# Mean over rows of 8192 on one core: a loop's 8 MB loads issued by GpSimd through the software queue

## The chip, the cores and the metric

The kernel runs on one core of a Trainium2 chip. A core has engines with instruction streams of their own: VectorE (DVE in the profile), ScalarE (ACT), GpSimd (POOL), SyncE (SP) and TensorE, which this kernel doesn't use. Sixteen DMA engines move data between the memory outside (HBM) and the core's on-chip memory (SBUF, 128 partitions). Engines issue DMAs; when one has landed, it raises a semaphore by 16, one for each DMA engine. The metric is the device time of one execution in microseconds (us), given as the median of several runs.

## What is computed

```python
def setup_inputs():
    return {"x": np.random.randn(64, 256, 8192).astype(np.float32)}

def reference(x):
    return np.mean(x, axis=2)
```

The input is 16,384 rows of 8192 floats, 536.9 MB; the output is one mean for each row, 64 KB. Each number is read once and added once.

## The kernel before

Rows are dealt to partitions so that a partition's rows lie one behind the other in memory: each partition owns 128 rows, 111 in a first zone and 17 in a second. A row is 32 KB, so one row for every partition is 4 MB. There are two landing buffers, `two` (two rows for each partition, 8 MB over all) and `four` (four rows, 16 MB).

The work goes through these buffers in turn. Ahead of the loop SyncE loads two single rows into `two` (three DMAs, lines 110 to 112) and four rows into `four` (line 113). Then come 17 rounds (`ROUNDS`) of six rows: two into `two` (line 117), four into `four` (line 119). Behind the loop stand five more loads of the same two sizes (`REST`, lines 122 to 128), two more 8 MB loads, and the last two rows in six pieces that get smaller and smaller.

All loads are issued by SyncE, in the order in which they are wanted, into one hardware queue. Ahead of each load SyncE waits until its buffer is free: for `two` until `two_free` is at least 1, which it then lowers by 1 (line 116); for `four` until `four_free` is at least 2, which it lowers by 2 (line 118).

VectorE sums the rows. `pair` (lines 169 and 170) sums both rows of `two` in one instruction and raises `two_free`. `quad` (lines 172 to 176) sums three rows of `four`, each by a `halves` (line 152) that adds the halves of a row and accumulates the result. ScalarE sums the fourth row of `four` at the same time (line 220, called in line 228). Both raise `four_free`.

VectorE's order is fixed by its program: in every round it waits for `two_sem` (line 184), does `pair`, waits for `go_sem`, which ScalarE raises when `four` has landed (lines 187 and 226), does `quad`, and copies three sums from a small tile to their place (line 190). So it takes `two` and `four` strictly in turn, whichever has landed.

GpSimd has little to do: at its start it raises `turn_sem`, and near the end it scales the first zone's 111 sums by 1/8192 (line 92, once `four_free` has reached 4), and later 16 of the second zone's (line 98).

Of the kernel before, what the change touches and what calls it, by code (L numbers as in the profile page):

```python
# [6 lines left out]
ADD = mybir.AluOpType.add  # L7
X = mybir.AxisListType.X
# [3 lines left out]
def bass_global_avg_pool_1d_kernel(  # L12
# [6 lines left out]
    B, C, L = x.shape  # L19
# [7 lines left out]
    ZONE = [111, 17]  # L27
    FROM = [0, ZONE[0]]
    EARLY, LATE = ZONE
    ROUNDS = (ZONE[0] - 9) // 6  # L30
# [16 lines left out]
    zone = [  # L47
        flat[P * f : P * (f + n), :].rearrange("(p r) l -> p (r l)", p=P)
        for f, n in zip(FROM, ZONE)
    ]  # L50
# [5 lines left out]
    with ExitStack() as ctx:  # L56
        sb = lambda n, s: ctx.enter_context(nc.sbuf_tensor(n, s, F32))
        sem = lambda n: ctx.enter_context(nc.semaphore(n))
# [8 lines left out]
        two = sb("two", [P, 2 * L])  # L67
# [3 lines left out]
        two_sem = sem("two_sem")  # L71
        turn_sem = sem("turn_sem")
        four_free = sem("four_free")
        two_free = sem("two_free")
# [4 lines left out]
        last_sem = sem("last_sem")  # L79
        pool_sem = sem("pool_sem")  # L80
        late_sem = sem("late_sem")
        out_sem = sem("out_sem")

        tail = four[:, 2 * L : 4 * L]
# [1 line left out]

        eng = nc.gpsimd
        eng.sem_inc(turn_sem, 2)  # L90
        eng.wait_ge(four_free, 4)
        eng.tensor_scalar(  # L92
            scaled[:], res[:, 0:EARLY], inv, None, op0=mybir.AluOpType.mult
# [8 lines left out]


        eng = nc.sync
        def rows_of(n, k):
            z = 1 if n >= FROM[1] else 0
            return zone[z][:, (n - FROM[z]) * L : (n - FROM[z] + k) * L]

        a, z = rows_of(ZONE[0] - 1, 1), rows_of(ZONE[0], 1)
        eng.dma_start(two[:, L : L + FIRST], z[:, 0:FIRST]).then_inc(first_sem, 16)  # L110
        eng.dma_start(two[:, L + FIRST : 2 * L], z[:, FIRST:L]).then_inc(first_sem, 16)
        eng.dma_start(two[:, 0:L], a).then_inc(first_sem, 16)
        eng.dma_start(four[:], rows_of(0, 4)).then_inc(second_sem, 16)
        src = rows_of(4, 6 * ROUNDS).rearrange("p (i w) -> p i w", i=ROUNDS)
        with eng.Fori(0, ROUNDS) as i:
            eng.wait_ge(two_free, 1).then_inc(two_free, -1)
            eng.dma_start(two[:], src[:, bass.ds(i, 1), 0 : 2 * L]).then_inc(two_sem, 16)
            eng.wait_ge(four_free, 2).then_inc(four_free, -2)
            eng.dma_start(four[:], src[:, bass.ds(i, 1), 2 * L : 6 * L]).then_inc(
                four_sem, 16  # L120
            )
# [12 lines left out]
        for c in range(6):  # L134
            a, z = cuts[c], cuts[c + 1]
# [12 lines left out]
        eng = nc.vector  # L148
# [16 lines left out]
        rows_in = lambda ap: ap.rearrange("p (j l) -> p j l", l=L)  # L165
        at = lambda n, k: res[:, n : n + k]
        sums = res[:, 4 : 4 + 6 * ROUNDS].rearrange("p (i w) -> p i w", i=ROUNDS)

        def pair(to, ap=two[:]):
            eng.tensor_reduce(to, rows_in(ap), X, ADD).then_inc(two_free, 1)  # L170

        def quad(to, done=four_free):
            for j, ap in enumerate(to):
                halves(
                    four[:, j * L : (j + 1) * L], ap, done if j == len(to) - 1 else None
                )

        eng.wait_ge(first_sem, 48)
        pair(at(ZONE[0] - 1, 2))
        eng.wait_ge(second_sem, 16)  # L180
        quad([at(j, 1) for j in range(3)])
        with eng.Fori(0, ROUNDS) as i:
            now = sums[:, bass.ds(i, 1), :]
            eng.wait_ge(two_sem, 16).then_inc(two_sem, -16)  # L184
            pair(now[:, :, 0:2])
            eng.wait_ge(go_sem, 1).then_inc(go_sem, -1)
            eng.wait_ge(turn_sem, 2).then_inc(turn_sem, -2)  # L187
            quad([turn[:, j : j + 1] for j in range(3)], turn_sem)
            eng.wait_ge(turn_sem, 1).then_inc(four_free, 1)
            eng.tensor_copy(  # L190
                now[:, :, 2:5], turn[:].rearrange("p (i w) -> p i w", i=1)
            ).then_inc(turn_sem, 1)
        for k, (n, size) in enumerate(REST):
            eng.wait_ge(two_sem if size == 2 else four_sem, 16 * (k // 2 + 1))
            if size == 4:
                quad([at(n, 1), at(n + 1, 1)])
            elif k < len(REST) - 1:
                pair(at(n, 2))
            else:
                pair(at(n, 1), two[:, 0:L])  # L200
# [16 lines left out]
        eng = nc.scalar  # L217
# [20 lines left out]
        for c in range(4):  # L238
            eng.wait_ge(chunk_sems[c], 16)
            a = cuts[c] if c else L  # L240
            ap = tail[:, a : a + mine[c]]
# [29 lines left out]
```

## Time and profile before

| what | value |
|---|---|
| time, median of 3 runs | 1243.4 us (1242.87 to 1243.65) |
| time of the profiled execution | 1242.81 us |
| its span in the profile | 1241.5 us |
| VectorE busy | 643.0 us |
| ScalarE busy | 176.6 us |
| GpSimd busy | 0.9 us |
| data moved | 536.94 MB, mean 433 GB/s |

The span runs from the first to the last recorded work; the device time has some 1.3 us more around it. In the profile's rows L152 is line 152 of the kernel; "SPq" is the instruction stream of SyncE, where DMA issues and waits stand. Of a DMA issue the profile gives the line, the buffer it writes and reads (`two<-in_x_dram`), how many there were, and the median time from issue to landing. A group's row gives what it wrote and read, the number of instructions, the busy time, the mean of one, and the idle time ahead of them with what ended it.

### The profile page before, as it was taken

The page shows a single profiled execution, that of the slowest core. Times are in us where ns is not written, and L with a number is a line of the kernel's source. Part 1 is how long each engine was busy: PE and PEld are TensorE (multiplying, and loading weights), DVE is VectorE, ACT ScalarE, POOL GpSimd, SP SyncE. Part 2 cuts the span into 40 slices and gives each one's busy share as a digit, 9 for nine tenths or more (in the row PEclk, how much of TensorE's full clock was granted, in tenths as well). Part 3 has the DMA queues.
Part 4 walks back from the last instruction along what each step waited for, and adds up shares of the span by engine and source line. Part 5 has one row for each costly group of instructions (what it writes and reads, how often), then busy time and mean ns, then how long its engine had stood idle before and what let it go on. Part 6 is the DMA issues. An engine that isn't in the chain of part 4 may idle for free. (4 is left out here: it accounts for less than half of the span.)

```text
span 1241.5 us, 715 instructions
## 1 busy us (share of the span) xinstructions
DVE 643.0 (52%) x168; ACT 176.6 (14%) x57; POOL 0.9 (0%) x6
## 2 busy tenths in 40 slices
DVE  2373836454544637383736454554638383725257
ACT  0011020202020202012020202020202102040423
POOL 0000000000000000000000000000000000000000
DMA  9999999999999999999999999999999999999998
GB/s 405 439 439 439 439 429 416 439 439 439 439 439 422 422 439 439 439 439 439 416 429 439 439 439 439 439 410 435 439 439 439 439 439 408 437 439 439 439 439 374
DMA packets 10192, 536.94 MB, mean 433 GB/s; under 512 B 1104, under 2 KB 1488, under 8 KB 1616
## 3 DMA queue, kind: packets, MB, share of 16 engines
q1 hardware_dynamic: 10192, 536.94, 99.9%
HBM read 536.87 MB, written 0.07 MB: 433 GB/s over the span
## 5 line engine op out<-in xcount | busy, mean ns | idle before, releaser
L152 DVE CUSTOM_DVE_ANT_0 four<-four 128x4096 f32<-128x4096 f32 (+4 forms) x63 | 260.7, 4184 | 434.9 <-DVEq L187 366.9
L170 DVE TENSOR_REDUCE res<-two 128x16384 f32 (+2 forms) x21 | 353.1, 16814 | 145.1 <-DVEq L184 96.2
L220 ACT ACTIVATE four<-four 128x8192 f32<-128x8192 f32 x22 | 154.7, 7030 | 1017.8 <-ACTq L226 864.3
L202 DVE TENSOR_REDUCE res<-four 128x2 f32<-128x16384 f32 x1 | 17.2, 17219 | 10.7 <-DMA four<-in_x_dram 10.7
L220 ACT ACTIVATE two<-two 128x8192 f32<-128x8192 f32 x2 | 14.1, 7032 | 36.7 <-DMA two<-in_x_dram 36.7
L206 DVE TENSOR_REDUCE res<-two 128x1 f32<-128x8192 f32 x1 | 8.7, 8686 | 2.1 <-DMA two<-in_x_dram 2.1
L242 ACT ACTIVATE four<-four 128x1984 f32<-128x1984 f32 (+3 forms) x4 | 4.3, 1064 | 7.8 <-DMA four<-in_x_dram 7.8
L190 DVE COPY res<-turn 128x3 f32 x17 | 2.9, 169 | 4.2 <-DVE turn L152 4.2
L152 DVE DVE_READ_ACCUMULATOR2_ANT turn<- 128x1 f32 x51 | 4.2, 82 | 0.0
L220 ACT ACTIVATION_READ_ACCUMULATOR four<-four (+1 forms) x22 | 4.1, 187 | 0.0
L220 ACT ACT_TABLE_LOAD x1 | 1.3, 1283 | 0.7 <-PEq L256 0.7
L92 POOL TENSOR_SCALAR scaled<-res 128x111 f32<-128x111 f32 x1 | 0.5, 505 | 1118.0 <-ACT four L220 1118.0
L242 ACT ACTIVATION_READ_ACCUMULATOR four<-four 128x1 f32 x4 | 0.8, 188 | 0.0
L152 DVE DVE_READ_ACCUMULATOR2_ANT res<- 128x1 f32 x8 | 0.7, 83 | 0.0
L220 ACT ACTIVATION_READ_ACCUMULATOR two<-two 128x1 f32 x2 | 0.4, 188 | 0.0
L98 POOL TENSOR_SCALAR ends<-res 128x16 f32<-128x16 f32 x1 | 0.3, 255 | 117.8 <-DVE res L152 117.8
L152 DVE DVE_READ_ACCUMULATOR2_ANT fin<- 128x1 f32 x4 | 0.3, 83 | 0.0
L152 DVE CUSTOM_DVE_ANT_0 fin<-fin 128x100 f32<-128x100 f32 x1 | 0.3, 264 | 0.0
L256 POOL MEMSET const-bfloat16-1.0<- 128x1 bf16 x1 | 0.1, 103 | 0.0
L256 POOL MEMSET const-uint8-127<- 128x1 uint8 x1 | 0.1, 102 | 0.0
L256 POOL MEMSET const-float32-0.0<- 128x1 f32 x1 | 0.1, 99 | 0.2 <-issue 0.2
L256 POOL MEMSET const-float32-1.0<- 128x1 f32 x1 | 0.1, 99 | 0.0
(1 smaller groups left out, 0.1 us busy)
## 6 DMA issues: line engine op xcount, KB each, us to landing
four<-in_x_dram SPq DMA_DIRECT2D x1, 5088.0 KB, 41.6
two<-in_x_dram SPq DMA_DIRECT2D x1, 4096.0 KB, 20.7
two<-in_x_dram SPq DMA_DIRECT2D x1, 3072.0 KB, 11.5
four<-in_x_dram SPq DMA_DIRECT2D x1, 2048.0 KB, 45.9
two<-in_x_dram SPq DMA_DIRECT2D x1, 1024.0 KB, 4.7
four<-in_x_dram SPq DMA_DIRECT2D x1, 640.0 KB, 47.0
four<-in_x_dram SPq DMA_DIRECT2D x21, 44.1
two<-in_x_dram SPq DMA_DIRECT2D x21, 40.3
```

The source lines that it names most:

```text
L92: eng.tensor_scalar(scaled[:], res[:, 0:EARLY], inv, None, op0=mybir.AluOpType.mult).then_inc(pool_sem, 1)
L98: eng.tensor_scalar(ends[:, 0 : LATE - 1], res[:, EARLY : OWN - 1], inv, None, op0=mybir.AluOpType.mult,).then_inc(late_sem, 1)
L152: made = eng.tensor_tensor_reduce(ap[:, 0:n], ap[:, 0:n], ap[:, n : 2 * n], scale=scale, scalar=0.0, op0=ADD, op1=ADD, accum_out=to,)
L170: eng.tensor_reduce(to, rows_in(ap), X, ADD).then_inc(two_free, 1)
L190: eng.tensor_copy(now[:, :, 2:5], turn[:].rearrange("p (i w) -> p i w", i=1)).then_inc(turn_sem, 1)
L202: eng.tensor_reduce(at(HALF, 2), rows_in(four[:, 0 : 2 * L]), X, ADD).then_inc(owned_sem, 1)
L206: eng.tensor_reduce(at(LASTP, 1), two[:, 0:L], X, ADD).then_inc(owned_sem, 1)
L220: return eng.activation(ap, ap, COPY, accum_out=to)
L242: eng.activation(ap, ap, COPY, accum_out=part(c)).then_inc(last_sem, 1)
L256: nc = _bacc.Bacc("TRN2", target_bir_lowering=False, num_devices=1)
```

## The change

GpSimd gets a loop of 17 rounds that issues the 8 MB loads of the loop, with `single_packet=True`: the eight runs of 64 KB that a DMA engine moves for such a load are marked as one packet. A DMA that GpSimd issues goes through the software queue. SyncE's loop keeps the 16 MB loads. Two semaphores are new: `loop_free`, which `pair` raises in the loop (and ahead of it) instead of `two_free`, and `soft_sem`, which the GpSimd loads raise. VectorE waits for `soft_sem` to reach 16 times the round's number, counted from 1, and doesn't lower it. After its loop GpSimd waits for the last `loop_free` and raises `two_free` by 1, so that SyncE's first 8 MB load behind the loop can start. All loads outside the loop stay with SyncE. What is loaded, where to, and how it is summed is the same.

```diff
+        loop_free = sem("loop_free")
+        soft_sem = sem("soft_sem")
...
+        def rows_of(n, k):
+            z = 1 if n >= FROM[1] else 0
+            return zone[z][:, (n - FROM[z]) * L : (n - FROM[z] + k) * L]
+
+        src = rows_of(4, 6 * ROUNDS).rearrange("p (i w) -> p i w", i=ROUNDS)
+
         eng = nc.gpsimd
         eng.sem_inc(turn_sem, 2)
+        with eng.Fori(0, ROUNDS) as i:
+            eng.wait_ge(loop_free, 1).then_inc(loop_free, -1)
+            eng.dma_start(
+                two[:], src[:, bass.ds(i, 1), 0 : 2 * L], single_packet=True
+            ).then_inc(soft_sem, 16)
+        eng.wait_ge(loop_free, 1)
+        eng.sem_inc(two_free, 1)
         eng.wait_ge(four_free, 4)
...
-        src = rows_of(4, 6 * ROUNDS).rearrange("p (i w) -> p i w", i=ROUNDS)
-        with eng.Fori(0, ROUNDS) as i:
-            eng.wait_ge(two_free, 1).then_inc(two_free, -1)
-            eng.dma_start(two[:], src[:, bass.ds(i, 1), 0 : 2 * L]).then_inc(two_sem, 16)
+        with eng.Fori(0, ROUNDS) as i:
             eng.wait_ge(four_free, 2).then_inc(four_free, -2)
             eng.dma_start(four[:], src[:, bass.ds(i, 1), 2 * L : 6 * L]).then_inc(
                 four_sem, 16
             )
...
-        def pair(to, ap=two[:]):
-            eng.tensor_reduce(to, rows_in(ap), X, ADD).then_inc(two_free, 1)
+        def pair(to, ap=two[:], free=two_free):
+            eng.tensor_reduce(to, rows_in(ap), X, ADD).then_inc(free, 1)
...
-        pair(at(ZONE[0] - 1, 2))
+        pair(at(ZONE[0] - 1, 2), free=loop_free)
...
-            eng.wait_ge(two_sem, 16).then_inc(two_sem, -16)
-            pair(now[:, :, 0:2])
+            eng.wait_ge(soft_sem, i * 16 + 16)
+            pair(now[:, :, 0:2], free=loop_free)
```

More of the change, by code (lines that the diff above doesn't have):

```diff
@@ L104, in bass_global_avg_pool_1d_kernel @@
         eng = nc.sync
-        def rows_of(n, k):
-            z = 1 if n >= FROM[1] else 0
-            return zone[z][:, (n - FROM[z]) * L : (n - FROM[z] + k) * L]
         a, z = rows_of(ZONE[0] - 1, 1), rows_of(ZONE[0], 1)
```

## The prediction

> **What bounds the kernel now.** I read the engine totals and the DMA part of the page first, to see which resource is full:
>
> ```profile
> span 1241.5 us, 715 instructions
> DVE 643.0 (52%) x168; ACT 176.6 (14%) x57; POOL 0.9 (0%) x6
> DMA  9999999999999999999999999999999999999998
> DMA packets 10192, 536.94 MB, mean 433 GB/s; under 512 B 1104, under 2 KB 1488, under 8 KB 1616
> q1 hardware_dynamic: 10192, 536.94, 99.9%
> ```
>
> VectorE (DVE) works half of the time, ScalarE (ACT) a seventh; the 16 DMA engines work 99.9% of it, all from one queue, q1. So the span is the time of the transfers, and a change can lengthen it only by making the DMA engines idle or slower. It can hardly shorten it: 0.1% of 1241.5 us is 1.2 us of idle.
>
> Next the loop by stages of one round, and the DMA view of two rounds:
>
> ```profile
> core 0: us, DVE busy (x) ACT busy (x) POOL busy (x), PEclk, DMA share, GB/s
> 190.80:248.70 57.90, 30.48 (x9) 7.12 (x2) 0.00 (x0) 1.00 1.00 434
> 248.70:306.70 58.00, 30.54 (x9) 7.12 (x2) 0.00 (x0) 1.00 1.00 434
> ```
>
> ```profile
> DMA packets 832, 50.33 MB, mean 434 GB/s; under 512 B 64, under 2 KB 64, under 8 KB 64
> four<-in_x_dram SPq DMA_DIRECT2D x2, 44.1
> two<-in_x_dram SPq DMA_DIRECT2D x2, 40.3
> ```
>
> A round takes 57.9 to 58.0 us at 434 GB/s. Of the 832 packets of two rounds 64 are tiny (four loads, 16 each); the other 768 share 50.33 MB, 64 KiB each. So an 8 MB load is 128 runs of 64 KiB, eight for each of 16 engines, and a 16 MB load sixteen for each. At 434 GB/s (one core's 8,388,608 and 16,777,216 bytes) that is 19.3 us and 38.7 us.
>
> Then the order of a round, from the timeline (start, duration, engine and line):
>
> ```profile
> 177.24 7.03 ACT L220 ACTIVATE four<-four 128x8192 f32<-128x8192 f32 x1 [50.88 <-ACTq L226]
> 177.38 4.43 DVE L152 CUSTOM_DVE_ANT_0 four<-four 128x4096 f32<-128x4096 f32 x1 [21.61 <-DVEq L187]
> ...
> 190.75 0.17 DVE L190 COPY res<-turn 128x3 f32 x1 [0.24 <-DVE turn L152]
> 190.80 0.38 SPq L119 DMA_DIRECT2D four<-in_x_dram  x1
> 196.53 17.22 DVE L170 TENSOR_REDUCE res<-two 128x16384 f32 x1 [5.61 <-DVEq L184]
> 213.99 0.33 SPq L117 DMA_DIRECT2D two<-in_x_dram  x1
> 235.18 7.03 ACT L220 ACTIVATE four<-four 128x8192 f32<-128x8192 f32 x1 [50.81 <-ACTq L226]
> 235.32 4.43 DVE L152 CUSTOM_DVE_ANT_0 four<-four 128x4096 f32<-128x4096 f32 x1 [21.57 <-DVEq L187]
> ```
>
> This is what keeps the DMA engines full with only two buffers. `four` lands at 177.2; VectorE takes 13.6 us over it and its next load is issued at 190.8. In these 13.6 us the DMA engines have work only because the 8 MB load of `two`, issued earlier, stands behind `four` in the same queue and so starts when `four` ends. `two` lands at 196.5, 5.7 us after `four` was re-issued; VectorE takes 17.2 us; `two` is re-issued at 214.0, while `four` streams until 235.2. Each load is covered by the one that was issued before it: first issued, first moved.
>
> **The change, part by part.**
>
> *Removed from SyncE (SP):* 17 waits on `two_free` and 17 issues. Their rows:
>
> ```profile
> SPq L118 <- SPq L118: 68.5, 2, 34.3
> SPq L116 <- SPq L116: 44.6, 2, 22.3
> ```
>
> In two rounds SP waits 113.1 us of 116 for buffers; it is never the reason why a load is late. Worth 0.
>
> *Added on GpSimd (POOL):* 17 waits on `loop_free` and 17 issues; after the loop one wait that hands the last `loop_free` on to `two_free`. Behind the waits on POOL stand only the later loads, the hand-over and the two small scalings, the first of which comes behind the loop as it is:
>
> ```profile
> POOL scaled L92 <- ACT four L220: 1118.0, 1, 1118.0
> ```
>
> The trace has no issue from POOL. From below, it costs what SP's does (0.33 us); from above, nothing is lost until the transfer starts so late that `two` lands after VectorE needs it. In the old order that slack is 235.2 − 214.0 = 21.2 us. I take 2 us and cost it at 0; the cover is the rest of the 16 MB load, and without it each microsecond would count 17 times. The hand-over delays the first 8 MB load behind the loop by less than a microsecond, under the same cover (the last 16 MB load of the loop is streaming): 0.
>
> *VectorE's waits* name `soft_sem` with a count that grows with the round, and no longer lower it. Behind each stand the pair, the quad and thus all of VectorE. The trace has no such wait; VectorE's own line-up, quad's end to the pair's start, is 5.6 us of waiting for data, so a fraction of a microsecond there is nothing: 0.
>
> *Moved past a queue:* this is the part that costs. The 8 MB loads leave q1, and with it their place behind the 16 MB load. The trace shows only one busy queue, so it can't show how an engine divides itself between two. Bounds: nothing, if the load in progress is finished first; or the whole cover, if the newcomer gets a share at once. I take the second: the loads are cut into 64 KiB packets in the records, so an engine has a place to change queues every 64 KiB of `four`, while the eight runs of `two` are now tied together.
>
> The Trainium skill speaks against the change here: "DMA: Bandwidth & Descriptors", section "Queues, rings and completion order", says that an engine takes turns between the queues that have work and changes only at the end of a packet. With one-run packets in q1 that gives the sum below; the same place calls 9 to 17 descriptors a typical packet, and with the whole 16 MB load as one packet it gives no change. No row here decides between the two.
>
> The round then runs as follows. Let `four` be issued at 0 with `two` already full. VectorE starts the pair at some 0.5 us and ends at 17.9; POOL issues `two`; its eight runs start at about 20 and pass `four`, which has some 20.7 us left. `two` lands at about 40 and lies unused, since VectorE's order has the quad next. `four` goes on and lands at about 60. Now both buffers are full and nothing is in flight: VectorE takes the quad, and the DMA engines idle until `four` is re-issued and its data starts.
>
> The price of one such gap: 13.6 us in the loop (177.24 to 190.80), 13.4 us before it, from these rows, in which the first load's landing time stands too:
>
> ```profile
> 61.04 7.03 ACT L220 ACTIVATE four<-four 128x8192 f32<-128x8192 f32 x1 [59.03 <-DMA four<-in_x_dram]
> 74.40 0.39 SPq L119 DMA_DIRECT2D four<-in_x_dram  x1
> ```
>
> ```profile
> two<-in_x_dram SPq DMA_DIRECT2D x1, 1024.0 KB, 4.7
> out_dram<-ends SPq DMA_DIRECT2D x1, 8.5 KB, 1.4
> ```
>
> and on top the part of issue-to-landing that isn't streaming: at most 4.7 − 2.4 = 2.3 us (1,048,576 bytes at 434 GB/s are 2.4 us), at least about 1.4 us (the 8.5 KB store, nearly all fixed). I take 1.9, the middle.
>
> How many: the quad ahead of the loop (its successor, the loop's first `two`, now passes it) and those of rounds 0 to 15. Round 16 is followed by an 8 MB load that SP issues into q1 behind `four`, as before. So 17. Sum: 13.4 + 16 × 13.6 = 231.0, plus 17 × 1.9 = 32.3, together 263.3 us. With 1.4 it is 254.8, with 2.3 it is 270.1. The profiled execution took 1242.8 us, 1.3 over its span, and the runs' median is 1243.4, 0.6 more: by the profiled execution 1242.8 + 263.3 = 1506 us, with 1498 and 1513 as ends. A round grows from 58 to 73.4 us.
>
> **The rivals.**
>
> *Order kept (not slower).* An engine finishes the load that it has begun before it looks at the other queue, because a load of q1 is one unit too, or because its runs have been taken in before POOL issues. For it: q1 shows no pause between loads, so runs are taken in well ahead. Against: the records count each 64 KiB by itself. Then `two` starts when `four` ends, as now, the 21.2 us of slack swallow the software's start, and `four`, re-issued 5.7 us before `two` lands, waits its turn behind a packet of eight runs. Price 0: 1243 us. It decides if at the moment of POOL's issue all that is left of `four`, about nine runs on each engine, counts as already begun; each run that doesn't lets `two` pass.
>
> *Even turns.* The flag does nothing and the queues alternate run by run. Then `two` needs 38.7 us from 20 and lands at 58.5; `four`, with 20.7 left, at 60: the same gap. But if POOL's issue is s us slower than SP's, `four` ends first and s − 1.4 us of `two` are left to fill the gap. With s up to 4 us, ten times SP's 0.38 us, the gap loses 2.6 us, 17 times 44 us: 1462 to 1506.
>
> *q1 first.* The software queue gets only what q1 leaves. Then `two` starts after `four`, but the re-issue of `four` 13.6 us later cuts it off some 4 us short, for 38.7 us, and VectorE waits for `two` with the pair next. After that the pair runs with both full: a gap of 17.2 + 2 = 19.2 us a round, 17 × 19.2 = 326, 1569 us. Nothing in the profile speaks for one queue over the other.
>
> *Faster.* Fewer pauses between packets, or transfers from two queues that overlap inside an engine. Against it: the engines are at 99.9%, and rounds run at 434 GB/s without a dip. All idle gone would give 1241.6 us; more needs a faster engine, of which nothing is seen.
>
> **How the numbers follow.** `two` passes `four`: 0.59, 1506 us. Even turns: 0.12, around 1484. q1 first: 0.03, 1569. Order kept: 0.21, 1243 us. Faster: 0.05, around 1241. A measurement of this kernel tells about 0.2%, 2.5 us, from no change. So faster 0.05, same 0.21, slower 0.74. The likeliest case with even turns beside it has 1462 to 1513, which I widen to 1525 for a slower start of VectorE's pair and wake-ups that add up over 17 rounds; that holds only 7 in 10. To leave out less than 2 in 10 the range has to reach the order that is kept: 1240 to 1525.
>
> **What would show it.** A second DMA queue with 17 × 8.39 = 142.6 MB, q1 with the remaining 394.3 MB. If `two` passes: rounds of 73 us; POOL's loads land 20 to 25 us after their issue in place of 40.3; SP's 16 MB loads land about 60 us after theirs in place of 44.1; VectorE starts the pair right after the quad instead of waiting 5.6 us, and waits about 42 us, not 21.6, ahead of the quad; the DMA share falls to some 83%, with a gap of 15 us in each round. If order is kept: rounds of 58 us, landing of 40 and 44 us as before. If turns are even: both loads land within 2 us of each other. If the rate inside a busy stretch is not 434 GB/s, the sum is wrong in a term that I hold fixed; if 8 MB loads start more than 18 us after the pair's end, POOL's issue is the cost that I put at nothing.

## The result, and the profile after

| what | before | after |
|---|---|---|
| time, median | 1243.1 us (1242.7 to 1243.65, 4 runs) | 1520.3 us (1519.43 to 1520.95, 4 runs) |
| ratio to before | | 1.223, 95% interval 1.2216 to 1.2245 |
| span of the profiled execution | 1241.5 us | 1518.2 us |

The change makes the kernel 22% slower. That is 277.2 us, or 16.3 us for each of 17 gaps.

The page of the changed kernel has the same compute and the same packets, but two queues (share of the 16 engines' span at the end of their rows):

```profile
span 1518.2 us, 753 instructions
DVE 642.9 (42%) x168; ACT 176.6 (12%) x57; POOL 10.1 (1%) x23
DMA packets 10192, 536.94 MB, mean 354 GB/s; under 512 B 1104, under 2 KB 1488, under 8 KB 1616
q1 hardware_dynamic: 7744, 394.33, 60.9%
q0 software_dynamic: 2448, 142.61, 21.7%
four<-in_x_dram SPq DMA_DIRECT2D x21, 60.5
two<-in_x_dram POOLq DMA_DIRECT2D x17, 42.3
```

60.9% and 21.7% are 82.6%: the DMA engines now stand still for a sixth of the time. Before, it was 99.9%. The 16 MB load takes 60.5 us from issue to landing (44.1 before). The 8 MB load takes 42.3.

The timeline of a round of the changed kernel (start, duration, engine and line):

```profile
240.03 0.17 DVE L198 COPY res<-turn 128x3 f32 x1 [0.24 <-DVE turn L160]
240.55 17.22 DVE L178 TENSOR_REDUCE res<-two 128x16384 f32 x1 [0.35 <-issue]
258.50 0.53 POOL L101 DMA_DIRECT2D two<-in_x_dram  x1 [73.66 <-POOLq L100]
301.13 7.03 ACT L228 ACTIVATE four<-four 128x8192 f32<-128x8192 f32 x1 [67.49 <-ACTq L234]
301.27 4.42 DVE L160 CUSTOM_DVE_ANT_0 four<-four 128x4096 f32<-128x4096 f32 x1 [43.51 <-DVEq L195]
...
314.70 0.37 SPq L127 DMA_DIRECT2D four<-in_x_dram  x1
315.15 17.22 DVE L178 TENSOR_REDUCE res<-two 128x16384 f32 x1 [0.34 <-issue]
```

VectorE starts the pair right behind the quad (0.35 us, 5.61 before), so `two` was already full. It then waits 43.5 us for `four` (21.6 before). `two` is issued at 258.5 and lands 42.3 us later, at about 300.8; `four` lands just before 301.1. Both come at the same moment, and nothing is in flight behind them. Stages of the same round, cut where the data ends and starts:

```profile
226.52:241.10 14.58, 13.85 (x8) 7.12 (x2) 0.00 (x0) 1.00 0.00 0
300.55:315.70 15.15, 13.84 (x8) 7.12 (x2) 0.00 (x0) 1.00 0.00 0
315.70:375.13 59.43, 16.67 (x1) 0.00 (x0) 0.53 (x1) 1.00 0.99 423
```

The DMA share is 0.00 for 15.15 us (the first row begins only at ScalarE's start, about 0.6 us after the last data). The stretch that follows moves a round's 25.2 MB in 59.43 us, 423 GB/s on the mean in place of 434. And this is how an engine divides itself while both loads are in flight, from 263.5 to 287.7 us:

```profile
DMA packets 160, 10.49 MB, mean 434 GB/s; under 512 B 0, under 2 KB 0, under 8 KB 0
q0 software_dynamic: 80, 5.24, 50.0%
q1 hardware_dynamic: 80, 5.24, 50.0%
```

These 24.2 us are ten run times (a run is the 64 KiB that an engine moves at once, 2.42 us), and 80 runs start from each queue, five for each of the 16 engines. The turns are even, although the kernel asks for the eight runs as one packet.

### The profile page after: what moved, and what is told of

Its sections match the earlier page's. It is cut to its first block, busy times and chain, and to the rows that moved or that the text cites. A ratio compares the mean times of both kernels' runs of the same rounds, so it can differ in the third digit from the quotient of the medians.

```text
span 1518.2 us, 753 instructions
## 1 busy us (share of the span) xinstructions
DVE 642.9 (42%) x168; ACT 176.6 (12%) x57; POOL 10.1 (1%) x23
## 3 DMA queue, kind: packets, MB, share of 16 engines
q1 hardware_dynamic: 7744, 394.33, 60.9%
q0 software_dynamic: 2448, 142.61, 21.7%
## 5 line engine op out<-in xcount | busy, mean ns | idle before, releaser
L101 POOL DMA_DIRECT2D two<-in_x_dram x17 | 9.2, 538 | 1216.6 <-POOLq L100 1216.6
## 6 DMA issues: line engine op xcount, KB each, us to landing
four<-in_x_dram SPq DMA_DIRECT2D x21, 60.5
two<-in_x_dram POOLq DMA_DIRECT2D x17, 42.3
```

The costliest lines, as they stand in the source:

```text
L101: eng.dma_start(two[:], src[:, bass.ds(i, 1), 0 : 2 * L], single_packet=True).then_inc(soft_sem, 16)
```

## The experiments

All times are medians. "Before" measured beside them was 1242.9 to 1243.0 us.

**The flag taken off.**

```diff
             eng.dma_start(
-                two[:], src[:, bass.ds(i, 1), 0 : 2 * L], single_packet=True
+                two[:], src[:, bass.ds(i, 1), 0 : 2 * L]
             ).then_inc(soft_sem, 16)
```

> The changed kernel without the single-packet flag. Theory (an engine takes turns between its two queues after every 64 KiB run, and the flag doesn't bind the eight runs): no change, 1517 to 1524 us, and both loads of a round still land within some 3 us of each other. Rival (the flag binds something, and the even turns seen come from another cause): the time moves by more than 5 us, or the 8 MB load's 42.3 us to landing moves by more than 3 us.

1520.45 us, ratio 1.223 (1.221 to 1.2251), the same as with the flag. The 8 MB load lands after 42.3 us, the 16 MB load after 60.6. The flag makes no difference that can be measured. Whether it reaches the DMA engines at all, the trace doesn't tell.

**The same loads through ScalarE's hardware queue.**

GpSimd's loop goes. ScalarE issues the first 8 MB load ahead of its own loop and the other 16 (`later`) in it; the fence shows the main part.

```diff
-        with eng.Fori(0, ROUNDS) as i:              # GpSimd's loop
...
+            # in ScalarE's loop, ahead of its wait for four_sem
+            eng.wait_ge(loop_free, 1).then_inc(loop_free, -1)
+            eng.dma_start(two[:], later[:, bass.ds(i, 1), 0 : 2 * L]).then_inc(
+                soft_sem, 16
+            )
```

> The loop's 8 MB loads are issued by ScalarE into its own hardware queue, at the same moments as GpSimd did. Theory (the cost is that there are two queues): 17 gaps as in the changed kernel; the issue starts data sooner than GpSimd's, which changes no gap: 1510 to 1525 us. Rival (the software queue itself costs: GpSimd's issue, the writing of descriptors): most of the 277 us comes back, 1243 to 1300 us.

1524.1 us, ratio 1.226 (1.2236 to 1.2285). The profile has no software queue at all, only two hardware ones:

```profile
q1 hardware_dynamic: 7744, 394.33, 60.7%
q10 hardware_dynamic: 2448, 142.61, 21.6%
two<-in_x_dram ACTq DMA_DIRECT2D x17, 42.8
```

So the loss needs neither the software queue nor GpSimd's issue. A second hardware queue costs as much, 3.8 us more even.

**GpSimd waits until the 16 MB load has landed.**

```diff
             eng.wait_ge(loop_free, 1).then_inc(loop_free, -1)
+            eng.wait_ge(landed, 1).then_inc(landed, -1)
             eng.dma_start(
...
             eng.sem_inc(go_sem, 1)
+            eng.sem_inc(landed, 1)
```

> GpSimd issues the 8 MB load only when the 16 MB load has landed, still through the software queue with the flag. Theory (the cost is that the 8 MB load enters while the 16 MB load is moving): first issued is first moved again, apart from the last stretch in which the re-issued 16 MB load shares; the only gap left is from landing to the 8 MB load's first data, 3 to 5 us, 17 times: 1295 to 1330 us, rounds of 61 to 63 us. Rival (the software queue itself is slow): a later issue can only make it worse, 1520 us or more.

1306.5 us, ratio 1.051 (1.0489 to 1.0531). The issue comes 17.3 us after the pair's end in place of 0.7, and the kernel is 214 us faster. The 8 MB load then takes 27.0 us to landing and the 16 MB load 47.9. The software queue with the flag is unchanged. What costs is that the 8 MB load enters while the 16 MB load is moving. What is left, 3.7 us a round, is 2.4 us without data between the two loads, and the cost of starting again that is measured further down. Here too the two loads share the engines, from the re-issue of the 16 MB load on, and the stretch (59.1 us) is no longer than with one queue that runs dry (59.2, below). So two queues with work at once are not what costs. Both buffers full at once are.

**Both loads of a round through the software queue, in the old order.**

```diff
             ).then_inc(soft_sem, 16)
+            eng.wait_ge(four_free, 2).then_inc(four_free, -2)
+            eng.dma_start(
+                four[:], src[:, bass.ds(i, 1), 2 * L : 6 * L], single_packet=True
+            ).then_inc(soft_four, 16)
...
```

SyncE's loop goes; behind it SyncE waits until GpSimd's loop is done. ScalarE waits for `soft_four` in place of `four_sem`.

> GpSimd issues both loads of every round, in the old order, both through the software queue with the flag; SyncE has none in the loop. Theory (only loads in different queues take turns, and the software queue is as quick as SyncE's): inside the loop first issued is first moved, rounds of 58 us; two gaps are left, at the loop's entry and its exit, where a load of one queue meets one of the other, 16 to 17 us each: 1270 to 1285 us. Rival (the software queue itself costs a part of the 277 us): over 1300 us, spread over all rounds.

1273.9 us, ratio 1.0247 (1.0217 to 1.0277), as expected: two gaps, each where a load of one queue meets one of the other. They are the only dips in the DMA share of the 40 slices (13.2 us without data near 80 us, 14.9 near 1080); in between, a round is as before, 57.96 us from one 8 MB issue to the next:

```profile
DMA  9959999999999999999999999999999999699999
229.04 0.57 POOL L103 DMA_DIRECT2D two<-in_x_dram  x1 [22.48 <-POOLq L102]
...
287.00 0.57 POOL L103 DMA_DIRECT2D two<-in_x_dram  x1 [22.46 <-POOLq L102]
```

Within the software queue too, first issued is first moved. The prediction's cost of nothing for GpSimd's issue holds.

**VectorE's stretch made shorter.**

```diff
-            quad([turn[:, j : j + 1] for j in range(3)], turn_sem)
+            quad([turn[:, j : j + 1] for j in range(2)], None)
+            halves(four[:, 2 * L : 2 * L + 256], turn[:, 2:3], turn_sem)
```

> In the loop's quad the third row's sum covers 256 of its 8192 numbers; the rest of that row is left out, so VectorE is some 4.1 us shorter over a 16 MB buffer (its 4.42 us instruction becomes one of about 0.3), and ScalarE's 7.0 us still ends earlier. Theory (the time is 17 gaps, and a gap is VectorE's stretch between landing and re-issue): the 16 gaps in the loop shrink by 4.1 us each, 66 us, to 1450 to 1460 us. Rival (the software loads themselves set the pace): VectorE's work is hidden, no change, 1520 us.

1453.8 us, ratio 1.1694 (1.1671 to 1.1718). That is 66.5 us less than the changed kernel's 1520.3, where 16 × 4.1 = 66 was expected. In the kernel before, with the DMA engines busy 99.9%, VectorE's work was hidden. In the changed kernel each microsecond of it between landing and re-issue counts.

**Shorter runs in the 16 MB load.**

```diff
-            eng.dma_start(four[:], src[:, bass.ds(i, 1), 2 * L : 6 * L]).then_inc(
-                four_sem, 16
-            )
+            for j in range(4):
+                eng.dma_start(
+                    four[:, j * L : (j + 1) * L],
+                    src[:, bass.ds(i, 1), (2 + j) * L : (3 + j) * L],
+                ).then_inc(four_sem, 16)
...
```

ScalarE waits for `four_sem` to reach 64 in place of 16.

> SyncE's 16 MB load of a round is issued as four loads of one row each, so its runs are 32 KiB in place of 64; GpSimd's loads stay as changed. Theory (turns are taken run by run, however long a run is): the 8 MB load gets two thirds of an engine, lands some 31 to 34 us after its issue in place of 42.3, ahead of the 16 MB load, and waits; the 17 gaps stay: 1510 to 1530 us. Rival (turns by bytes or by time): still 42 us to landing.

1517.1 us, ratio 1.2204 (1.2168 to 1.2239). The 8 MB load now lands first, after 33.2 us in place of 42.3. A stretch in which both loads move (264 to 288 us):

```profile
DMA packets 224, 10.98 MB, mean 457 GB/s; under 512 B 1, under 2 KB 1, under 8 KB 1
q0 software_dynamic: 112, 7.34, 70.5%
q1 hardware_dynamic: 112, 3.64, 35.1%
```

As many runs from the one as from the other, though q0's are twice as long: turns are counted in runs, not in bytes. The time hardly moves, since `two` landing early only lies there until the quad has been done.

**Very short runs in the 8 MB load, with the flag and without.**

```diff
-                two[:], src[:, bass.ds(i, 1), 0 : 2 * L], single_packet=True
+                two[:], src[:, bass.ds(i, 1), 0 : 2 * L],
+                max_dma_last_dim=4096, single_packet=True,
```

> GpSimd's 8 MB loads are cut into runs of 16 KiB, 32 for an engine, still with the flag; SyncE's runs stay 64 KiB. Theory (turns run by run, and the flag binds nothing): the 8 MB load gets a fifth of an engine while the 16 MB load ends (20.7 us of it take 26), and has 14 us left, which fill the 15 us gap: 1243 to 1265 us. Rival (the flag binds an engine's runs to one packet that isn't interrupted): the 8 MB load passes and lands in 22 to 25 us, 17 gaps, 1500 to 1525 us.

> The same 16 KiB runs without the flag. Theory: as with the flag, within 5 us. Rival (the flag binds): only this one falls to 1243 to 1265 us, and the one with the flag stays above 1500 us.

1609.8 us with the flag and 1609.1 without, ratios 1.2949 (1.2911 to 1.2987) and 1.2944 (1.2906 to 1.2981). Both numbers missed the expectation. The limit counts bytes, not elements: the runs became 4 KiB, not 16. The flag does nothing here either. While both loads move (303 to 339.3 us), the first of the two shows:

```profile
DMA packets 475, 16.69 MB, mean 460 GB/s; under 512 B 0, under 2 KB 0, under 8 KB 235
q1 hardware_dynamic: 240, 15.73, 100.0%
q0 software_dynamic: 235, 0.96, 6.4%
```

A 4 KiB run for a 64 KiB run: the 8 MB load gets a seventeenth of the bytes and is starved as long as the 16 MB load moves. It lands 62.3 us after its issue, behind the 16 MB load, so VectorE, whose next work is the pair, makes the DMA engines wait for that instead:

```profile
266.42:286.00 19.58, 19.58 (x2) 2.94 (x2) 1.14 (x1) 1.00 0.00 0
286.00:346.50 60.50, 10.88 (x8) 4.06 (x1) 0.00 (x0) 1.00 0.99 416
```

This is the gap that the prediction's rival "q1 first" priced at 19.2 us. Here it comes of short runs, though; no run shows an engine that puts one queue first.

**The runs that were meant: 32 KiB and 16 KiB**, with the same edit and limits of 32768 and 16384.

> GpSimd's 8 MB loads in runs of 32 KiB, with the flag; SyncE's runs stay 64 KiB. Theory (turns run by run): the 16 MB load's last 20.7 us take 31, the 8 MB load moves 10.3 us of its 19.3 in them and has 9 us left, which fill a part of the 15.2 us gap; 6.2 us idle and 1.4 us of uneven ends a round: 1243 + 17 x 7.6 = 1372 us, 1345 to 1395. Rival (what decides is only that there are two queues, and not the length of the runs): 1520 us.

> The same with runs of 16 KiB, the size that was meant in the two runs whose records show 4 KiB. Theory: the 16 MB load's last 20.7 us take 26, the 8 MB load has 14 us left and fills all but a microsecond of the gap, and lands just as the re-issued 16 MB load starts: 1243 + 17 x 1 to 2.4 = 1260 to 1285 us, 1245 to 1300. Rivals: 1520 us if the length of the runs doesn't matter; some 1600 us, as with 4 KiB, if the load is still unfinished when the 16 MB load is issued again.

1357.4 us with 32 KiB, ratio 1.0921 (1.0889 to 1.0953). 1277.9 us with 16 KiB, ratio 1.0281 (1.0251 to 1.0311). Both lie in the ranges given. With the queues, the issue times and the flag unchanged, the length of the runs alone takes back up to 242 us. The 8 MB load's time to landing is 42.2 and 41.9 us, as in the changed kernel (42.3); the 16 MB load's is 50.9 and 46.2 us in place of 60.5, because fewer bytes pass it. What is left of the 8 MB load then fills the gap. With 32 KiB some 5.5 us a round are left without data. With 16 KiB the pair waits just 0.75 us for the load:

```profile
246.57 4.43 DVE L161 CUSTOM_DVE_ANT_0 four<-four 128x4096 f32<-128x4096 f32 x1 [28.38 <-DVEq L196]
...
260.00 0.37 SPq L128 DMA_DIRECT2D four<-in_x_dram  x1
260.86 17.22 DVE L179 TENSOR_REDUCE res<-two 128x16384 f32 x1 [0.75 <-DMA two<-in_x_dram]
```

What is left with 16 KiB, 2 us a round, is 0.6 us without data (260.4 to 261.0) and, again, the cost of starting, which the next run measures.

**One queue that runs dry.** On the mean, the changed kernel's stretches between gaps are slow, 423 GB/s for 434. Taking turns could be the reason, or starting again from nothing. So the kernel before, with its one queue, got the late issue (ScalarE raises `landed`, as above):

```diff
             eng.wait_ge(two_free, 1).then_inc(two_free, -1)
+            eng.wait_ge(landed, 1).then_inc(landed, -1)
             eng.dma_start(two[:], src[:, bass.ds(i, 1), 0 : 2 * L]).then_inc(two_sem, 16)
...
```

> The kernel before, all loads in SyncE's one queue, but in the loop SyncE issues the 8 MB load only when the 16 MB load has landed: the DMA engines run dry once a round, for some 1.7 us (landing to issue to first data), and start again, and no two queues ever take turns. It tells where the changed kernel's slower stretches (423 GB/s for 434, some 1.4 us a round) come from. If from taking turns: 17 x 1.7 us, about 1272 us, 1265 to 1282, and 434 GB/s between the gaps. If from starting again after running dry: 17 x 3.1 us, about 1296 us, 1288 to 1305, and 423 GB/s between the gaps.

1293.5 us, ratio 1.0405 (1.0375 to 1.0436), the value for starting again:

```profile
243.33:245.01 1.68, 0.99 (x1) 1.06 (x1) 0.00 (x0) 1.00 0.00 0
245.01:304.22 59.21, 29.52 (x8) 6.06 (x2) 0.00 (x0) 1.00 0.99 425
```

One queue, no turns, and still 59.2 us at 425 GB/s where a round that never runs dry takes 57.95. So it is starting again that costs. The trace of the changed kernel shows where. Here are two stretches of one run time each, the first right behind a gap, the second 10 us later:

```profile
315.70:318.12 2.42, 2.42 (x1) 0.00 (x0) 0.00 (x0) 1.00 1.35 433
326.00:328.42 2.42, 2.42 (x1) 0.00 (x0) 0.00 (x0) 1.00 1.00 433
```

In each of them 16 runs start, one for each engine, and the DMA share (last but one) counts the whole time of the runs that start. So a run behind the gap takes 1.35 × 2.42 = 3.3 us, a later one 2.42, as in the kernel before, where the share is 1.00. The rate isn't lower. The first run of each engine takes some 0.8 us longer, and most of the rest is that the engines start and end up to 0.4 and 0.8 us apart. Why a first run takes longer isn't shown.

## Why the prediction was right, and where it was off

The direction, the place and the size hold: 1520.3 us measured, 1506 predicted, inside 1240 to 1525. The range says little, since it reaches from no change to the likeliest case. That case's own ends are 1498 and 1513, and the upper one is 7 us short of the measured time. Point by point:

- *The bound.* "A change can lengthen it only by making the DMA engines idle or slower." Confirmed. The busy time of VectorE is the same to 0.1 us, and the DMA share fell from 99.9% to 82.6%.
- *Parts costed at 0* (SP's waits, GpSimd's issue, VectorE's new wait). Confirmed by the run with both loads through GpSimd, which has the counting waits too and rounds of 58 us.
- *The gap and its count.* 13.6 + 1.9 = 15.5 us was predicted, and 15.15 us of full idle was measured in the loop. The trace has 17 such gaps, one behind the quad ahead of the loop and one in each of rounds 0 to 15. That the gap is made of VectorE's stretch was shown by shortening the quad.
- *"`two` lands at about 40 and lies unused."* This step failed. I took it that the eight runs, tied together, pass `four` and land 20 to 25 us after their issue. They took 42.3 us: the flag made no difference and the queues alternated run by run, which was the rival "even turns", to which I gave 0.12 against 0.59. The time hardly tells the two apart, since the gap opens whenever both buffers are full at once; the runs of 32 KiB in the 16 MB load made `two` pass, and took 1517 us. So the number doesn't bear this step out. That the wrong order of landing cost it nothing was luck, as far as the reading of the flag goes; the rival itself said "the same gap".
- *The rival's own price* (1462 to 1506) was too low because it let a late start of GpSimd's load shorten the gap by up to 2.6 us. GpSimd's issue itself takes 0.53 us, and the gap is full length.
- *The 1.9 us on top of VectorE's stretch* is the term that was mis-sized. A round shows 15.15 us of idle and then 59.43 us for a round's bytes in place of 57.95, 16.6 us more in all, of which 13.6 is VectorE's stretch: so about 3 us in place of 1.9, above the 2.3 that the sum took as the most. 1.6 of it is idle before VectorE starts and after the re-issue, as the sum had it; the other 1.5 is the slow first run of each engine and their uneven start and end, which it didn't have. Over the 17 gaps, the first of them shorter, the mean is (277.2 − 231.0) / 17 = 2.7 us. That is the 14 us between 1506 and 1520. The rate, which the prediction named as a term that it held fixed, did hold: 2.42 us a run behind the first.
- *Order kept* was ruled out: a load that has begun is not finished first. An engine changes queues behind each run of 64 KiB, so each counts as a packet of its own. Read so, that agrees with the Trainium skill, "DMA: Bandwidth & Descriptors", section "Queues, rings and completion order", that an engine changes queues at the end of a packet. It doesn't agree with the page's 9 to 17 descriptors as a typical packet: here the engines took turns after one run, of 4 KiB as well as of 64, and with the flag too, and the runs decide.
- *Faster* had no room: no run came below the kernel before.

## What to carry to other kernels

Where buffers are few and loads are wanted in turn, a single queue's first-in, first-out order is itself what hides the compute: here, moving one stream of loads to another queue made the loads share the engines, both buffers were full at the same time, and the compute between landing and re-issue became idle time of the DMA engines. Look at what each load is covered by, not only at how busy its queue or its issuer is. If two queues must be used, issue when the transfer in progress is done, or set the shares by the length of the runs; here 16 KiB against 64 KiB gave back 242 of 277 us, while 4 KiB went too far and took 1610 us.

## What the runs showed that I had not expected

- The single-packet flag had no effect on a software load: 1520.3 and 1520.45 us with runs of 64 KiB, 1609.8 and 1609.1 us with runs of 4 KiB.
- Two busy queues took turns one run each, with runs of 4 to 64 KiB: 80 runs against 80 at equal length, 112 against 112 at 64 and 32 KiB, 235 against 240 at 4 and 64 KiB. So the length of its runs set a queue's share.
- DMA engines that ran dry lost 1.3 to 1.5 us in the stretch that followed, beyond the idle time itself (59.21 and 59.43 us for a round's bytes, 57.95 without). The loss is in the first run of each engine, 3.3 us in place of 2.42, and in uneven starts and ends; the later runs are as quick as ever.
- Loads of 8 and 16 MB were as quick through the software queue as through the hardware queue: rounds of 57.96 us with all loads of the loop issued by GpSimd, 57.95 with SyncE.
